# The first two columns of a norm weight fetched by GpSimd, its whole turned later, and 17 fillers in place of 13 in a one-core encoder layer

## The chip, the core and the metric

The kernel runs on one core of a Trainium2 chip. The metric is the device time of one execution in microseconds (us), taken as the median of several executions; less is better. Engines are named as the profile names them: PE (TensorE matmul) with PEld (its weight loads), DVE (VectorE), ACT (ScalarE), POOL (GpSimd) and SP (SyncE). ACT, SP and POOL also issue DMAs; a "q" behind a name (ACTq, SPq, POOLq) marks such an issue.

## What is computed

One layer of a bidirectional encoder: RMS norm, one projection, two head groups (attention and a gated linear recurrence), and an output projection with a residual. Only the beginning matters here:

```
def rms_norm(x, w):                       # x: 512 x 2048, w = norm_w: 2048
    y = x * rsqrt(mean(x * x, -1) + EPS)
    return y * w

h = rms_norm(x, norm_w)
proj = einsum('bsd,de->bse', h, w_in)     # w_in: 2048 x 4608
q, k, v, g_attn, xr, g_lru = split(proj)  # xr is projected first here
...
return x + einsum('bse,ed->bsd', mixed, w_out)
```

## The kernel before

The 2048 channels are handled in 16 blocks of 128, two blocks to a chunk `c` of 256 channels. A matmul contracts over the partitions, so each 128x128 square of x has to be turned (transposed by PE against the identity matrix `ident`) before it can be used. `xturn` (L226) turns one block: four transposes into one PSUM tile, then ACT writes the block scaled by its column of `norm_w` and rounded to the short float32 format (`xh`, L232), and DVE writes what the rounding left (`xl`, L233). The row factor of the norm is applied after the projection. `wsplit` (L198) splits a weight tile in the same way: ACT casts (`wh`, L204), DVE subtracts (`wl`, L205). Each product is then three matmuls: high x high, high x low, low x high.

The scaling needs one column of `norm_w` per block, that is, each channel's value on its own partition. Before, `norm_w` comes in as 16 rows of 128 (`nw_st`, 16 descriptors of 512 B, L937, on ACT's queue between the two halves of the first weight tile), and `columns` (L175) turns it whole with one small PE transpose (L179) and a DVE copy (L181) into `nw`, 128x16.

While nothing has arrived, PE multiplies a tile of ones with itself (`busy`, L921, the "fillers": 128x256 in bfloat16, L923): `WARM` = 13 of them at the very beginning, and `WARM2` = 6 between the first turned block and the first product. The ones are set by GpSimd (L153), behind the identity's first instruction.

PE's order is the order in which the code is written. It begins: 13 fillers, turn of `norm_w`, turn of block 0, 6 fillers, four products of block 0 (L287: high x high for four column blocks), turn of block 1, the other products of blocks 0 and 1, then chunk after chunk (L145 to L147). At the beginning ACT, DVE and SP keep the written order as well. Each waits on semaphores, in order; what stands behind a waiting instruction on its engine waits too. The lines of the setup are 934 to 955:

```
    with tc.high_priority():
        xs, ws = xload(0, 2), wraw(w_in, 0, C_XR, 2, nc.scalar)
        xc, raw = next(xs), next(ws)
        nc.scalar.dma_start(nw_st, norm_w.rearrange("(k p) -> k p", p=P))
        next(xs), next(ws)
        ...
        columns(nw, nw_st)
        first = [wsplit(raw, 0)]
        xturn(xc, 0)
        busy(WARM2)
```

`xload(0, 2)` brings chunk 0 of x in two halves of 256 KB on SP's queue (block 0, then block 1); `wraw(..., 2, nc.scalar)` brings the first weight tile in two halves of 256 KB on ACT's queue.

Of the kernel before, what the change touches and what calls it, by code (L numbers as in the profile page):

```python
# [12 lines left out]
AF = mybir.ActivationFunctionType  # L13
ALU = mybir.AluOpType
AX = mybir.AxisListType

P = 128
# [19 lines left out]
AHEAD = 600  # L37


WARM, WARM2 = 13, 6  # L40


STEPS = 2
# [12 lines left out]
def hybrid_kernel(  # L56
# [20 lines left out]
    nc = tc.nc  # L77
# [34 lines left out]
    def x2():  # L112
        return pools["xw"].tile([P, SEQ], F32R, tag="x2", bufs=32, name=nm("x2"))
# [21 lines left out]
    def mm():  # L135
        return ps.tile([P, SEQ], F32, tag="mm", name=nm("mm"))

    def const(shape, name, dt=F32):
        return cp.tile(list(shape), dt, tag=name, name=name)

    def f(ap):
        return ap.bitcast(F32)
# [7 lines left out]
    ident = const([P, P], "ident")  # L150
    make_identity(nc, ident)
    ones = const([P, P], "ones")
    nc.gpsimd.memset(ones, 1.0)  # L153
    nhalf = const([P, 48], "nhalf")
    nc.gpsimd.memset(nhalf, -0.5)

    nw_st = const([KT, P], "nw_st")
    vec_st = const([R_END, P], "vec_st")

    def vec_load():  # L160
        for lo, src in (
            (R_CW, conv_w.rearrange("t o (n p) -> (t o n) p", p=P)),
            (R_CB, conv_b.rearrange("(n p) -> n p", p=P)),
            (R_BA, lru_ba.rearrange("d (n p) -> (d n) p", p=P)),
            (R_BX, lru_bx.rearrange("d (n p) -> (d n) p", p=P)),
            (R_LAM, lru_lambda.rearrange("d (n p) -> (d n) p", p=P)),
            (R_AN, attn_norm_w.rearrange("(n p) -> n p", p=P)),
            (R_LN, lru_norm_w.rearrange("(n p) -> n p", p=P)),
        ):
            nc.sync.dma_start(vec_st[lo : lo + src.shape[0], :], src)  # L170

    nw = const([P, KT], "nw")
    vec = const([P, R_END], "vec")

    def columns(dst, src):  # L175

        n = src.shape[0]
        pt = mm()
        nc.tensor.transpose(pt[:, :n], src, ident[:n, :n])  # L179
        with tc.high_priority():  # L180
            nc.vector.tensor_copy(dst, pt[:, :n])  # L181
# [5 lines left out]
    def wraw(w, r0, c0, nk=1, queue=nc.sync):  # L187

        raw = pools["wr"].tile([P, 2, SEQ], F32, tag="wr", bufs=3, name=nm("wr"))
        src = w[r0 : r0 + 2 * P, c0 : c0 + SEQ].rearrange("(k p) e -> p k e", p=P)  # L190
        for k in range(nk):
            ks = slice(k * 2 // nk, (k + 1) * 2 // nk)
            queue.dma_start(raw[:, ks, :], src[:, ks, :])
            yield raw
# [3 lines left out]
    def wsplit(raw, k):  # L198

        turn_of[0] += k  # L200
        pool = pools["wx" if "wx" in pools and turn_of[0] % 2 else "xw"]
        hi = pool.tile([P, SEQ], F32R, tag="wh", bufs=4, name=nm("wh"))
        lo = pool.tile([P, SEQ], F32R, tag="wl", bufs=4, name=nm("wl"))
        nc.scalar.copy(hi, raw[:, k, :])  # L204
        nc.vector.tensor_sub(lo, raw[:, k, :], f(hi))  # L205
        return hi, lo

    def wload(w, r0, c0):
        with tc.high_priority(AHEAD):
            (raw,) = wraw(w, r0, c0)  # L210
            return [wsplit(raw, k) for k in range(2)]


    xh, xl = [None] * KT, [None] * KT
    ssq = const([P, NT, KT // 2], "ssq")

    def xload(c, nk=1):

        xc = b4(shape=(P, NT, 2 * P))
        for k in range(nk):  # L220
            ks = slice(k * 2 * P // nk, (k + 1) * 2 * P // nk)
            cs = slice(c * 2 * P + ks.start, c * 2 * P + ks.stop)
            nc.sync.dma_start(xc[:, :, ks], xf[:, cs].rearrange("(t p) d -> p t d", p=P))
            yield xc

    def xturn(xc, kk):  # L226
        pt = mm()
        for t in range(NT):
            ks = slice(kk % 2 * P, (kk % 2 + 1) * P)
            nc.tensor.transpose(pt[:, t * P : (t + 1) * P], xc[:, t, ks], ident)  # L230
        xh[kk], xl[kk] = x2(), x2()
        nc.scalar.activation(xh[kk], pt, AF.Identity, scale=nw[:, kk : kk + 1])  # L232
        nc.vector.scalar_tensor_tensor(  # L233
            xl[kk], pt, nw[:, kk : kk + 1], f(xh[kk]), op0=ALU.mult, op1=ALU.subtract
        )

    def xsquare(xc, c):
        for t in range(NT):
            nc.vector.scalar_tensor_tensor(
                xc[:, t, :], xc[:, t, :], 1.0, xc[:, t, :], op0=ALU.mult, op1=ALU.mult,  # L240
                accum_out=ssq[:, t, c : c + 1],
            )

    def xchunk(c):
        with tc.high_priority(AHEAD):
            (xc,) = xload(c)
        yield
        with tc.high_priority(AHEAD):
            for k in range(2):
                xturn(xc, 2 * c + k)  # L250
        xsquare(xc, c)
        yield
# [17 lines left out]
    def xstats():  # L270
        s = const([P, NT], "xsum")
        nc.vector.reduce_sum(s, ssq, axis=AX.X)
        rsqrt_mean(rstd, s, DM, NT)
        rows(rbc, rstd, k2(shape=(P, NT, P)))
# [3 lines left out]
    def proj_feat(c0, acc, first=None, given={}):  # L278

        acc += [pj() for _ in range(4)]  # L280
        for c in range(KT // 2):
            if c == 0 and first:

                for k, (wh, wl) in enumerate(first):
                    for j, (w, x_) in enumerate(((wh, xh), (wl, xh), (wh, xl))):
                        for e in range(4):
                            nc.tensor.matmul(  # L287
                                acc[e], w[:, e * P : (e + 1) * P], x_[k],
                                start=k == 0 and j == 0, stop=False,
                            )  # L290
                            if (j, e) in ((1, 1), (2, 3)):
                                yield c, 2 * k + j - 1
                        if (k, j) == (0, 0):
                            yield None
                continue
            ws = given[c] if c in given else wload(w_in, c * 2 * P, c0)
            for e in range(4):
                es = slice(e * P, (e + 1) * P)
                for k, (wh, wl) in enumerate(ws):
                    kk = 2 * c + k  # L300
                    mm3(acc[e], wh[:, es], wl[:, es], xh[kk], xl[kk], kk == 0, kk == KT - 1)
                yield c, e
# [618 lines left out]
    def busy(n):  # L921
        for _ in range(n):
            nc.tensor.matmul(warm[:, : 2 * P], wv[:, :P], wv, start=True, stop=True)  # L923
# [10 lines left out]
    with tc.high_priority():  # L934
        xs, ws = xload(0, 2), wraw(w_in, 0, C_XR, 2, nc.scalar)
        xc, raw = next(xs), next(ws)
        nc.scalar.dma_start(nw_st, norm_w.rearrange("(k p) -> k p", p=P))  # L937
        next(xs), next(ws)
        table = const([P, 1], "table")
        nc.scalar.activation(table, ones[:, :1], AF.Exp)  # L940
        columns(nw, nw_st)
        first = [wsplit(raw, 0)]
        xturn(xc, 0)
        busy(WARM2)
    chunks = [xchunk(c) for c in range(1, KT // 2)]
    loads, turns = iter(chunks), iter(chunks)
    for step in proj_feat(C_XR, a1, first, given):
        if step is None:
            with tc.high_priority():
                first.append(wsplit(raw, 1))  # L950
                xturn(xc, 1)
            xsquare(xc, 0)
            next(next(loads), None)
            given[1] = wload(w_in, 2 * P, C_XR)
            continue
        c, e = step
        if (e == 0 or e == 2) and c:
            next(next(loads, iter(())), None)
        if (e, c) == (2, 0) or (e == 1 and c) or (e, c) in ((3, 1), (3, 2)):
            next(next(turns, iter(())), None)  # L960
        if (c, e) == (1, 2):
            given[2] = wload(w_in, 4 * P, C_XR)
            s2.close()
        if (c, e) == (2, 3):
            vec_load()
        if (c, e) == (5, 3):
            columns(vec, vec_st)
        if (c, e) == (KT // 2 - 1, 0):
            with tc.high_priority():
                xstats()  # L970
# [171 lines left out]
```

## Time and profile before

| | us |
|---|---|
| three executions | 663.28, 663.50, 661.22 |
| median | 663.28 |
| the profiled execution: its own time | 663.34 |
| the profiled execution: span, first to last instruction | 661.5 |

So 1.8 us of the profiled execution's time lie outside its span. Every time below counts from the start of that span. PE is busy for 654.1 us of the span in 3067 matmuls, DVE 490.6, ACT 346.0, POOL 91.8. A row of the timeline reads: start, duration, engine, line, operation, output<-inputs, shapes, count, and in brackets the idle time of the engine before it with what ended it. Rows of one kind that follow each other are merged into one (x13). A matmul's duration runs from its issue to its modelled end, so durations of neighbours overlap; the pace is read from starts, or from the chain of waits, which has no overlaps.

### The profile page before, as it was taken

What the parts mean: (1) busy time and instruction counts of PE and PEld (TensorE: products, weight loads), DVE (VectorE), ACT (ScalarE), POOL (GpSimd) and SP (SyncE); (2) the same over time, 40 slices, a digit from 0 to 9 for tenths busy, and PEclk for the clock granted to TensorE, in tenths of its full rate; (3) what the DMA queues carried; (4) which work ended last, traced back from release to release, by engine and by line L of the source; (5) the groups of instructions that cost most, each with busy time, mean ns of one, the idle gap of its engine ahead of it and who ended that gap; (6) DMA issues with size and microseconds to landing.
All of it is one profiled execution on the core that took longest, in us unless ns stands there. A gap on an engine that the chain in (4) does not pass through costs nothing.

```text
span 661.5 us, 8826 instructions
## 1 busy us (share of the span) xinstructions
PE 654.1 (99%) x3067; PEld 540.6 (82%) x3067; DVE 490.6 (74%) x851; ACT 346.0 (52%) x639; POOL 91.8 (14%) x121
## 2 busy tenths in 40 slices
PE   8999999999999999999999999999999999999997
PEld 6888888888888888888888888888888878888875
DVE  4879688977687952855865569528967998698994
ACT  3543799489856514454644437435444564333441
POOL 0000000000012301223253335410000000010000
PEclk9999999999999999999999999999999999999999
DMA  8843252322334221345776768762355766585322
GB/s 289 272 143 96 65 141 90 97 64 64 83 106 151 81 90 32 97 138 149 152 168 164 216 128 180 176 153 79 89 164 207 264 215 216 211 290 192 125 83 95
DMA packets 52732, 96.19 MB, mean 145 GB/s; under 512 B 4184, under 2 KB 14544, under 8 KB 52560
## 3 DMA queue, kind: packets, MB, share of 16 engines
q1 hardware_dynamic: 45648, 75.17, 36.0%
q0 software_dynamic: 6720, 19.93, 13.1%
q10 hardware_dynamic: 320, 0.53, 0.3%
q8 instruction: 24, 0.39, 0.2%
q14 instruction: 20, 0.16, 0.1%
HBM read 91.42 MB, written 20.97 MB: 170 GB/s over the span
## 4 chain that ended last, share of the span: by engine, by line
PE 88%; DVE 4%; issue 3%; DMA 3%; POOL 1%; ACT 0%; DVEq 0%; ACTq 0%; POOLq 0%
PE pj L145 19%; PE pj L147 19%; PE pj L146 19%; PE mm L890 9%; PE pj L890 7%; PE mm L146 3%; PE mm L147 3%; PE mm L145 3%; DVE ol L705 2%; PE mm L575 2%; DMA rw<-ts 2%; PE mm L230 1%; PE pj L287 1%; PE mm L523 1%; DMA nw_st<-in_norm_w_dram 1%
## 5 line engine op out<-in xcount | busy, mean ns | idle before, releaser
L145 PE MATMUL pj<-x,wh 128*128 128x512 f32 x376 | 150.2, 400 | 0.0
L147 PE MATMUL pj<-x,wl 128*128 128x512 f32 x376 | 147.1, 391 | 0.0
L146 PE MATMUL pj<-x,wh 128*128 128x512 f32 x376 | 146.7, 390 | 0.0
L204 ACT CAST wh<-wr 128x512 fp32r<-128x512 f32 x144 | 86.5, 617 | 75.9 <-PE pj L147 29.0
L205 DVE TENSOR_TENSOR wl<-wr,wh 128x512 fp32r<-128x512 f32 x144 | 99.5, 711 | 30.7 <-ACT wh L204 30.5
L147 PEld LDWEIGHTS pj<-x,wl 128*128 128x128 f32 x376 | 70.6, 188 | 15.4
L146 PEld LDWEIGHTS pj<-x,wh 128*128 128x128 f32 x376 | 70.8, 188 | 14.0 <-issue 0.5
L145 PEld LDWEIGHTS pj<-x,wh 128*128 128x128 f32 x376 | 70.7, 188 | 13.8 <-issue 0.5
L145 PE MATMUL pj<-wh,x 128*128 128x512 f32 x192 | 75.7, 394 | 0.0
L146 PE MATMUL pj<-wl,x 128*128 128x512 f32 x192 | 75.3, 392 | 0.0
L147 PE MATMUL pj<-wh,x 128*128 128x512 f32 x192 | 75.2, 392 | 0.0
L704 ACT CAST oh<-rw 128x512 fp32r<-128x512 f32 x94 | 54.8, 619 | 31.8 <-PE mm L890 14.5
L705 DVE TENSOR_TENSOR ol<-rw,oh 128x512 fp32r<-128x512 f32 x94 | 60.6, 686 | 9.2 <-ACT oh L704 6.8
L890 PE MATMUL mm<-ol,mh 128*128 128x512 f32 x128 | 50.2, 392 | 0.5 <-DVE ol L705 0.5
L890 PE MATMUL mm<-oh,mh 128*128 128x512 f32 x128 | 50.3, 393 | 0.0
L890 PE MATMUL mm<-oh,ml 128*128 128x512 f32 x128 | 50.2, 392 | 0.0
L577 ACT CAST b<-mm 128x512 fp32r<-128x512 f32 x32 | 18.7, 585 | 58.7 <-PE mm L575 58.7
L563 DVE TENSOR_REDUCE mx<-mm 128x1 f32<-128x512 f32 x32 | 22.0, 688 | 31.2 <-PE mm L147 30.9
L145 PEld LDWEIGHTS pj<-wh,x 128*128 128x128 f32 x192 | 36.1, 188 | 8.1 <-issue 0.2
L146 PEld LDWEIGHTS pj<-wl,x 128*128 128x128 f32 x192 | 36.1, 188 | 8.1 <-issue 0.2
L147 PEld LDWEIGHTS pj<-wh,x 128*128 128x128 f32 x192 | 36.1, 188 | 7.9
L890 PE MATMUL pj<-oh,mh 128*128 128x512 f32 x96 | 37.8, 394 | 0.0
(207 smaller groups left out, 1153.7 us busy)
## 6 DMA issues: line engine op xcount, KB each, us to landing
wr<-in_w_in_dram SPq DMA_DIRECT2D x71, 512.0 KB, 3.7
rw<-in_w_out_dram SPq DMA_DIRECT2D x63, 256.0 KB, 3.9
ts<-in_w_out_dram POOLq DMA_DIRECT2D x24, 512.0 KB, 6.9
rw<-ts SPq DMA_DIRECT2D x31, 256.0 KB, 5.0
ts<-ts POOLq DMA_DIRECT2D x8, 512.0 KB, 5.7
xt<-in_x_dram SPq DMA_DIRECT2D x8, 512.0 KB, 8.2
b<-in_x_dram SPq DMA_DIRECT2D x7, 512.0 KB, 7.7
out_dram<-xt POOLq DMA_DIRECT2D x12, 256.0 KB, 3.0
```

The lines of the kernel that those rows point to most:

```text
L145: nc.tensor.matmul(acc, lh, rh, start=start, stop=False)
L146: nc.tensor.matmul(acc, lh, rl, start=False, stop=False)
L147: nc.tensor.matmul(acc, ll, rh, start=False, stop=stop)
L204: nc.scalar.copy(hi, raw[:, k, :])
L205: nc.vector.tensor_sub(lo, raw[:, k, :], f(hi))
L230: nc.tensor.transpose(pt[:, t * P : (t + 1) * P], xc[:, t, ks], ident)
L563: nc.vector.tensor_reduce(mx, sc, axis=AX.X, op=ALU.max, negate=True)
L575: nc.tensor.transpose(pt[:, s * P : (s + 1) * P], p[:, s * P : (s + 1) * P], ident)
L577: nc.scalar.copy(pth[:, :, tt], p3)
L704: nc.scalar.copy(hi, src)
L705: nc.vector.tensor_sub(lo, src, f(hi))
L890: nc.tensor.matmul(bank[name, s], lh[:, a, ts_], rh, start=i == 0 and j == 0, stop=i == 7 and j == 2,)
```

## The change

- `nw2`, a new 128x2 tile, takes the first two columns of `norm_w` straight from memory: GpSimd issues a DMA of 128x2 single elements (256 pieces of 4 bytes). Blocks 0 and 1 are scaled with `nw2`, all others with `nw` as before.
- `norm_w` as 16 rows (`nw_st`) is issued behind the second half of the first weight tile on ACT's queue; its turn and copy (`columns`) stand behind the turn of block 1.
- `WARM` is 17 in place of 13.
- The ones are set by VectorE instead of GpSimd.

```
-WARM, WARM2 = 13, 6
+WARM, WARM2 = 17, 6
...
-    nc.gpsimd.memset(ones, 1.0)
+    nc.vector.memset(ones, 1.0)
...
     nw = const([P, KT], "nw")
+    nw2 = const([P, 2], "nw2")
...
-        nc.scalar.activation(xh[kk], pt, AF.Identity, scale=nw[:, kk : kk + 1])
+        w = (nw2 if kk < 2 else nw)[:, kk : kk + 1]
+        nc.scalar.activation(xh[kk], pt, AF.Identity, scale=w)
         nc.vector.scalar_tensor_tensor(
-            xl[kk], pt, nw[:, kk : kk + 1], f(xh[kk]), op0=ALU.mult, op1=ALU.subtract
+            xl[kk], pt, w, f(xh[kk]), op0=ALU.mult, op1=ALU.subtract
         )
...
         xc, raw = next(xs), next(ws)
+        nc.gpsimd.dma_start(nw2, norm_w[: 2 * P].rearrange("(k p) -> p k", p=P))
+        next(xs), next(ws)
         nc.scalar.dma_start(nw_st, norm_w.rearrange("(k p) -> k p", p=P))
-        next(xs), next(ws)
         table = const([P, 1], "table")
         nc.scalar.activation(table, ones[:, :1], AF.Exp)
-        columns(nw, nw_st)
         first = [wsplit(raw, 0)]
...
                 first.append(wsplit(raw, 1))
                 xturn(xc, 1)
+                columns(nw, nw_st)
```

What stands in a row on the engines is shown at three places. A row reads: line, operation, output<-inputs, shape, and the semaphores that it waits for; DMAHW0, DMAHW1, ... count the transfers of the SP and ACT queues in turn, eight counts that are used again, and DMASW0 that of GpSimd. Line numbers of the changed kernel are one to three higher.

The first place is PE's start. Before, from the last filler of the first group to the first filler of the second; `b_18_139` is chunk 0 of x:

```order
L923 MATMUL mm_118<-ones 128x256
L179 MATMUL mm_148<-ident,nw_st 128x16 [waits DMAHW2_49,Pool_49]
L230 MATMUL mm_155<-ident,b_18_139 128x128 [waits DMAHW1_49]
L230 MATMUL mm_155<-ident,b_18_139 128x128 x3
L923 LDWEIGHTS ones
```

Now the same stretch:

```order
L925 MATMUL mm_119<-ones 128x256
L231 MATMUL mm_158<-ident,b_18_144 128x128 [waits DMAHW1_49,Pool_49]
L231 MATMUL mm_158<-ident,b_18_144 128x128 x3
L925 LDWEIGHTS ones
L925 MATMUL mm_119<-ones 128x256
```

And PE now from the last of the first four products of block 0 on (`mm_185` is block 1 turned):

```order
L289 MATMUL pj_176<-x_23_163,wh_154 128x512
L231 MATMUL mm_185<-ident,b_18_144 128x128 [waits DMAHW3_49]
L231 MATMUL mm_185<-ident,b_18_144 128x128 x3
L180 MATMUL mm_194<-ident,nw_st 128x16 [waits DMAHW4_49]
L289 MATMUL pj_173<-x_23_163,wl_155 128x512 [waits DVE_49]
```

The turn of `nw_st` has left the place ahead of block 0, and with it the wait for its transfer; it now stands behind the turn of block 1, ahead of the products with `wl`.

The second place is ACT's start. Before:

```order
L193 DMA wr_141<-in_w_in_dram 128x512
L937 DMA nw_st<-in_norm_w_dram 16x128
L193 DMA wr_141<-in_w_in_dram 128x512
L940 ACT_TABLE_LOAD
L940 ACTIVATE table<-ones 128x1 [waits Pool_49]
L204 CAST wh_151<-wr_141 128x512 [waits DMAHW0_49]
L232 ACTIVATE x_24_160<-mm_155,nw 128x512 [waits DVE_49,PE_49]
L204 CAST wh_178<-wr_141 128x512 [waits DMAHW4_49]
```

Now; `nw_93` is `nw2`:

```order
L194 DMA wr_146<-in_w_in_dram 128x512 x2
L941 DMA nw_st<-in_norm_w_dram 16x128
L943 ACT_TABLE_LOAD
L943 ACTIVATE table<-ones 128x1 [waits DVE_49]
L205 CAST wh_154<-wr_146 128x512 [waits DMAHW0_49]
L234 ACTIVATE x_23_163<-mm_158,nw_93 128x512 [waits DMASW0_49,PE_49]
L205 CAST wh_181<-wr_146 128x512 [waits DMAHW2_49]
```

`nw_st` is issued third instead of second, and the scaling of block 0 waits for GpSimd's transfer where it waited for DVE's copy.

The third place is POOL's start. Before:

```order
masks.py:197 MEMSET ident 128x128
L153 MEMSET ones 128x128
masks.py:199 ISA
masks.py:199 AFFINE_SELECT ident<-ident 128x128 [waits Pool_49]
L155 MEMSET nhalf 128x48
```

Now:

```order
L939 DMA nw_93<-in_norm_w_dram 128x2x1
masks.py:197 MEMSET ident 128x128
L155 MEMSET nhalf 128x48
masks.py:199 ISA
masks.py:199 AFFINE_SELECT ident<-ident 128x128 [waits Pool_49]
```

The DMA stands ahead of the identity, and the memset of the ones is gone from here; it is now DVE's first instruction.

## The prediction

> **What bounds the kernel now.** I read the shares by engine first, then the chain of waits of the first 16 us in order of time, then single engines. From the page:
>
> ```profile
> PE 654.1 (99%) x3067; PEld 540.6 (82%) x3067; DVE 490.6 (74%) x851; ACT 346.0 (52%) x639; POOL 91.8 (14%) x121
> PEclk9999999999999999999999999999999999999999
> PE 88%; DVE 4%; issue 3%; DMA 3%; POOL 1%; ACT 0%; DVEq 0%; ACTq 0%; POOLq 0%
> ```
>
> PE holds 88% of the chain, so a microsecond that PE gains at the start is carried to the end, unless something behind it is not ready. The change touches only the start. The chain there (start, duration, what):
>
> ```profile
> 0.72 0.45 ACTq L193
> 1.17 0.03 issue
> 1.20 4.21 DMA nw_st<-in_norm_w_dram
> 5.41 0.14 issue
> 5.54 0.26 PE mm L179
> 5.80 1.05 PE mm L230 x4
> 6.84 1.28 PE mm L923 x6
> 8.12 1.71 PE pj L287 x4
> 9.83 0.54 PE mm L230 x4
> 10.37 3.23 PE pj L287 x14
> 13.60 0.87 PE mm L230 x8
> 14.47 1.38 PE pj L287 x6
> ```
>
> Two things are to be seen. The norm weight's rows, issued at 1.20, land at 5.41, and PE starts on them alone. And the pace doubles: four products take 1.71 us (0.43 each), the 14 after 10.37 take 3.23 (0.23 each); four turns take 1.05, then eight 0.87. The rise lies near 9.9. The page's clock row shows 9 in every slice, so it does not show this; the paces do.
>
> Now PE and ACT themselves, by the timeline:
>
> ```profile
> 1.12 2.95 PE L923 MATMUL mm<-ones 128*128 128x256 bf16 x13 [1.12 <-POOL ones L153]
> 5.54 0.26 PE L179 MATMUL mm<-ident,nw_st 16*128 16x16 f32 x1 [1.46 <-DMA nw_st<-in_norm_w_dram]
> 5.73 1.12 PE L230 MATMUL mm<-ident,b 128*128 128x128 f32 x4
> 7.78 2.06 PE L287 MATMUL pj<-x,wh 128*128 128x512 f32 x4
> 13.44 1.04 PE L230 MATMUL mm<-ident,b 128*128 128x128 f32 x8
> 19.21 0.48 PE L145 MATMUL pj<-x,wh 128*128 128x512 f32 x1
> ```
>
> ```profile
> 6.88 0.69 ACT L232 ACTIVATE x<-mm,nw 128x512 fp32r<-128x512 f32 x1 [1.66 <-PE mm L230]
> 7.47 0.61 ACT L204 CAST wh<-wr 128x512 fp32r<-128x512 f32 x1
> 14.07 1.27 ACT L232 ACTIVATE x<-mm,nw 128x512 fp32r<-128x512 f32 x2 [1.95 <-PE mm L230]
> ```
>
> PE is busy from 1.12 to 4.07, idle for 1.46, then busy without a break. So 2.95 us of work without a break did not bring the rise, and the 4.3 to 4.4 us from 5.54 on did.
>
> **Part 1: the first turn starts earlier.** When is x there? SP's rows:
>
> ```profile
> 5.02 0.51 SPq L193 DMA_DIRECT2D wr<-in_w_in_dram  x1
> 8.12 2.15 SPq L170 DMA_DIRECT2D vec_st<-in_conv_w_dram  x1
> b<-in_x_dram SPq DMA_DIRECT2D x2, 256.0 KB, 4.6
> ```
>
> The DMA at 5.02 waits, by the program, for the same count (DMAHW1) as PE's turn of block 0. So block 0 is there by 5.0, and nw_st by 5.4 was the last. From landing to PE went 0.13 (5.41 to 5.54). The earliest new start is 5.1. Against it stand 256 extra pieces and a second weight half that now follows the first without nw_st between; nothing in the trace shows their price. The bounds are nothing and what block 1 shows, 4.6 us from its issue near 1.2, so 5.8. I take 5.25, nearest to the row that is the same transfer: 0.48 earlier than 5.73.
>
> **Part 2: 17 fillers and VectorE's ones.** GpSimd's row for the ones is 0.20 from 0.86, behind the identity's; on DVE nothing is ahead, so 0.72 + 0.20, and PE starts near 1.0 instead of 1.12.
>
> ```profile
> 0.72 0.20 POOL masks.py:197 MEMSET ident<- 128x128 f32 x1 [0.29 <-POOLq L1127]
> 0.86 0.20 POOL L153 MEMSET ones<- 128x128 f32 x1
> 1.36 0.13 POOL L155 MEMSET nhalf<- 128x48 f32 x1
> ```
>
> At 2.95/13 = 0.227 each, 17 take 3.86 and end at 4.85, before the turn at 5.25: they delay nothing, and the gap shrinks from 1.46 to 0.4. If the rise needs L us of unbroken work, L lies between 2.95 and 4.4. Fillers of 3.86 reach it over 0.91 of these 1.45 us, and if a gap of 0.4 does not undo what went before, everywhere: the rise comes between 1.0 + 2.95 = 3.95 and 1.0 + 4.4 + 0.4 = 5.8. This is the larger term.
>
> **Part 3: the sum** at the fast pace, row by row. Turn at 5.25; ACT's scaling 0.63 later (13.44 to 14.07), at 5.88; it ends at 6.57 (0.69); the first product 0.2 later (before: 7.57 to 7.78), at 6.77. Six fillers fit in between, since they need half of 1.28. Four products: 0.25 for the first (0.48 against 0.23, row 19.21) and 4 x 0.23; turn of block 1, half of 0.87; turn of nw_st, 0.2 (5.54 to 5.73). That is 6.77 + 0.25 + 0.92 + 0.44 + 0.2 = 8.58, where before it was 10.37: 1.79 less. With the rise only at 5.8, turn and scaling go at the old distance (5.73 to 6.88, 1.15), and it is about 1.3 less. I take **1.7**, near the first, since most of 3.95 to 5.8 lies before the turn.
>
> **Part 4: what must be hidden.** The new transfer, first of all. The groups of GpSimd's DMAs (count; busy, mean ns), then the landing times by line, in the same order:
>
> ```profile
> L738 POOL DMA_DIRECT2D ts<-in_w_out_dram x16 | 17.4, 1089 | 49.3 <-issue 39.5 <-DVE ev L632 4.8 <-DVE mx L563 4.8
> L735 POOL DMA_DIRECT2D ts<-in_w_out_dram x8 | 6.2, 780 | 2.8 <-issue 2.8
> L825 POOL DMA_DIRECT2D out_dram<-xt x12 | 6.6, 554 | 197.3 <-DVE xt L861 145.9 <-DMA rw<-in_w_out_dram 23.4 <-DVE xt L866 23.2
> DMA to landing us min/median/max: 6.3/7.2/8.9
> DMA to landing us min/median/max: 3.9/4.9/8.4
> DMA to landing us min/median/max: 2.5/2.9/5.6
> ```
>
> L735 and L738 move 512 KB in 256 rows, as many pieces as nw2 has (L738 adds to what is there); the stores, L825, 256 KB in 128 rows. nw2 has 1 KB. ACT needs it at 5.88, that is 5.16 after its issue at 0.72. Bounds: 2.5 to 8.9; I take 4, above the stores' median since it has twice the pieces among busy queues, and below L735's since few bytes are to be moved: there at 4.7, with 1.2 to spare. The identity waits behind this issue: 0.72 + 1.09 at most + the 0.77 of the rows from 0.72 to 1.49 makes 2.6, under the fillers; without that cover it would cost 1.9.
>
> A price that only the notes state: the Trainium skill, "DMA: Bandwidth & Descriptors" (Anatomy of one DMA), gives about 2 us fixed for a DMA issued by GpSimd, so about 2.7 as an estimate; no run here has such a small one, and the sum would stay the same.
>
> nw_st now lands behind the second weight half. That half is there by 8.12 (the load of vec_st waits for it) and by ACT's cast at 7.47; its issue is 0.55 earlier now. nw_st is needed at 8.4. Bounds: nothing, or a few tenths if it comes after 8.4; I take nothing. DVE's copy (0.17) moves in between; its first reader, ACT's scaling of chunk 1, comes at 14.07 - 1.8 = 12.3, about 2 us after. SP's load of chunk 4 now waits for the weight half, at most 2 us later than 5.57; chunk 4 is turned at 25.7. Choosing nw2 or nw is free.
>
> The profiled execution took 663.34, of which 661.5 is span: 663.34 - 1.7 = **661.6**. The median, 663.28, is the same within 0.06.
>
> **Rivals.**
>
> *The rise does not come earlier* (chance 0.24). If it needs more than 3.86 us and any gap starts it anew, it comes 4.3 after the new start, as before. Then only the start remains: 0.48 less, 662.9. For it: one break of 1.46 did undo 2.95 us of work. Against it: most of the values of L that the trace allows are below 3.86. The Trainium skill, "TensorE: Matmul & The Clock Gate" (Part 1), has a rule that speaks for this rival: the rise follows a window of 3.4 us at a phase free of the kernel's start that was busy throughout. By that, 3.86 us hold a whole window in about one start of eight; by its wording of a busy window with a threshold it does not name, more. The rise at 9.9 agrees with such windows, and does not tell the threshold.
>
> *The small transfer is late* (slower; 0.09). Its place is ACT L232, with the cast of the second weight half queued behind it, and all products behind both. Landing after L738's longest, 8.9, is 9.62: ACT starts 2.74 later than at 6.88. If the faster pace is there by then, four products give 0.8 back: +1.9, 665.2. It decides from a landing at 6.9 on the span's clock without the early rise, at 7.7 with it. For it: 4-byte pieces among queues that are full. Against it: the stores' median of 2.9.
>
> *It does not do what it says* (0.08): pushed by the new pieces, block 0 comes at 5.6 or later, the gap is 0.8 or more and the rise stays: 663.3.
>
> **How the numbers follow.** Forecast 0.55, with a range of its own from 661.3 to 662.4. About 0.04 is left for causes that I don't see. The range from 660.2 to 664.0 takes in the forecast and the rivals at 662.9 and 663.3; below, it allows for scatter, one execution of before having been 2 us under the others; the late transfer is left out. A measurement of this kernel tells about 0.5% (3.3 us) from no change. No case gives 3.3 us less by its rows: the whole wait and the whole slow pace are hardly more than 2.3; scatter leaves 0.06 for faster. Slower by 3.3 needs a landing at 10 or later: 0.03. Within 0.5%: 0.91.
>
> **What would show it.** First turn of block 0 between 5.1 and 5.5, with at most 0.6 of idle time before it, ended by the transfer of x: part 1. The first four products in about 0.95 on the chain, not 1.71: part 2; if they take 1.7, the first rival. ACT's first scaling released by PE: part 4 right; by the DMA of nw2: the second. The block of 14 products starting near 8.6. PE waiting at the turn of nw_st, or at chunk 1 for DVE, would make the prediction wrong in a way that I priced at nothing.

## The result, and the profile after

| | median, us | all executions, us | ratio to before |
|---|---|---|---|
| before, in the same job | 663.11 | 661.22 to 664.40 (22) | |
| the changed kernel | 663.88 | 663.70 to 665.59 (22) | 1.0019 [1.0012, 1.0025] |

The change costs 0.8 us: within 0.5% of before, but on the other side of it than the forecast of 661.6. The executions of the changed kernel fall in two groups, 17 of 22 at 663.7 to 664.0 and 5 at 665.3 to 665.6; the profiled one (665.36, span 663.6) belongs to the second. No execution of the first group was traced, so what sets the two apart can only be argued from other kernels' traces, below.

The chain of waits of its start (start, duration, what):

```profile
1.29 5.96 DMA nw<-in_norm_w_dram
...
7.34 0.70 ACT x L234
...
8.08 1.97 PE pj L289 x4
10.05 0.85 PE mm L231 x4
10.90 0.21 PE mm L180
11.12 3.67 PE pj L289 x14
```

It begins with the small transfer, `nw2` (the profile leaves out the numbers in names and writes `nw`). Its issue starts at 1.29, not at 0.72, it lands at 7.25, and ACT's first scaling waits for it. The four products take 1.97 and the 14 products start at 11.12; before, it was 10.37.

PE and ACT by the timeline:

```profile
1.04 3.81 PE L925 MATMUL mm<-ones 128*128 128x256 bf16 x17 [1.04 <-DVE ones L153]
5.36 0.63 PE L231 MATMUL mm<-ident,b 128*128 128x128 f32 x4 [0.51 <-DMA b<-in_x_dram]
5.82 0.82 PE L925 MATMUL mm<-ones 128*128 128x256 bf16 x6
8.08 1.97 PE L289 MATMUL pj<-x,wh 128*128 128x512 f32 x4 [1.44 <-ACT x L234]
```

```profile
7.34 0.69 ACT L234 ACTIVATE x<-mm,nw 128x512 fp32r<-128x512 f32 x1 [2.22 <-DMA nw<-in_norm_w_dram]
```

Everything up to the first turn is as forecast. The fillers run from 1.04 to 4.85, and block 0 is turned at 5.36 after a gap of 0.51 that x's transfer ends. The turn takes 0.63 where it took 1.12, and six fillers take 0.82, so the fast pace is there. Then ACT sits idle for 2.22 and PE for 1.44. And the pace is lost again, as the windows show (first column the window, last three the granted clock, the DMA share, which is printed a little above 1 where the engines are full, and GB/s):

```profile
8.00:9.00 1.00, 0.92 (x3) 0.73 (x4) 0.94 (x2) 0.53 (x2) 0.00 (x0) 0.61 1.04 380
9.00:10.00 1.00, 1.00 (x4) 0.70 (x3) 0.41 (x1) 0.00 (x0) 0.00 (x0) 0.50 1.09 356
...
11.00:12.00 1.00, 1.00 (x4) 0.82 (x5) 0.34 (x1) 1.00 (x2) 0.00 (x0) 0.68 1.10 354
```

The clock is at half between two changes: 0.61 over the first microsecond puts the fall at 8.22, and 0.68 over the last the rise at 11.64. The clock records that are kept with the trace have the same two, and an earlier rise at 4.81.

### The profile page after: what moved, and what is told of

The parts are those of the page before. It is cut to its first block, busy times and chain, and to the rows that moved or that the text cites. A ratio compares the mean times of both kernels' runs of the same rounds, so it can differ in the third digit from the quotient of the medians.

```text
span 663.6 us, 8840 instructions
## 1 busy us (share of the span) xinstructions
PE 655.9 (99%) x3071; PEld 540.5 (81%) x3071; DVE 491.0 (74%) x852; ACT 346.5 (52%) x639; POOL 93.0 (14%) x121
## 4 chain that ended last, share of the span: by engine, by line
PE 96%; DMA 1%; DVE 1%; issue 1%; ACT 0%; DVEq 0%; ACTq 0%; POOLq 0%
PE pj L147 20%; PE pj L145 20%; PE pj L146 20%; PE mm L892 12%; PE pj L892 9%; PE mm L147 3%; PE mm L146 3%; PE mm L145 3%; PE mm L577 2%; PE pj L289 1%; PE mm L231 1%; DMA nw<-in_norm_w_dram 1%; PE mm L525 1%; DMA rw<-in_w_out_dram 1%; DVE ol L707 0%
## 5 line engine op out<-in xcount | busy, mean ns | idle before, releaser
L892 PE MATMUL pj<-ol,mh 128*128 128x512 f32 x96 | 37.8, 394 | 0.0
```

The source lines that it names most:

```text
L892: nc.tensor.matmul(bank[name, s], lh[:, a, ts_], rh, start=i == 0 and j == 0, stop=i == 7 and j == 2,)
```

## The experiments

Theory: the gains of the forecast came, and two costs ate them, the late transfer and one outside the start. Rivals: the early pace does not come or is worth nothing; or moving `nw_st` or GpSimd's part of the work costs something of its own. Each job timed the kernel before beside its kernels; "against before" is the difference to that median. Line numbers of after hold for its variants; those of before, for its variants (one more where a tile is added).

**a1_ones_scale.** The changed kernel with blocks 0 and 1 scaled by ones (it leaves `norm_w` out of these two blocks); the transfer is issued, and nobody waits for it.

```
-        w = (nw2 if kk < 2 else nw)[:, kk : kk + 1]
+        w = ones[:, :1] if kk < 2 else nw[:, kk : kk + 1]
```

> The changed kernel, with blocks 0 and 1 scaled by a column of ones instead of nw2: the norm weight is left out for these two blocks, the small DMA is still issued and nobody waits for it. Theory A (the late landing of nw2, 7.25 us in the changed kernel, ate the gain): ACT's first scaling starts within 0.7 us of the turn's start, near 6.0, the chain's 14 products start near 8.7 instead of 11.1, no fall of the clock, and the time is about 1.7 us under the kernel before: ratio 0.997 to 0.998. Rival B (the fillers or the 256 pieces cost the time themselves, by the clock or by pushing x): ACT starts early, and yet the time stays within 0.5 us of before or above.

Measured: 662.49 (662.17 to 662.99, 11 executions), before 662.89, ratio 0.9997 [0.9989, 1.0006]. Its chain:

```profile
0.73 4.15 DMA b<-in_x_dram
...
5.01 0.65 PE mm L231 x4
...
5.68 0.70 ACT x L234
...
6.42 1.21 PE pj L289 x4
...
8.06 0.16 PE mm L180
8.22 3.40 PE pj L289 x14
```

This is the start that the forecast worked out: x's transfer first, then no wait but ACT's scaling; the turn of `nw_st` waits for nothing. The 14 products start at 8.22 (forecast 8.58; before 10.37). Yet of these 2.15 us the median keeps 0.40, which cannot be told from nothing. Something after the start takes back well over 1 us.

**a2_before_17.** The kernel before with 17 fillers, nothing else.

```
-WARM, WARM2 = 13, 6
+WARM, WARM2 = 17, 6
```

> The kernel before with 17 fillers and nothing else. Theory of the clock (unbroken work of about 3.4 us brings the rise; short breaks do not undo it): the rise comes before 6 us in most executions, the four first products take 0.95 us on the chain, and the time is 1.0 to 1.4 us under before, ratio 0.998 to 0.9985. Rival (the earlier rise is lost again in the gap between the fillers and the first product, as in the changed kernel's profile): ratio 0.9995 to 1.001, with a fall of the clock in the profile.

Measured: 662.79, before 662.89, ratio 0.9996 [0.9985, 1.0006], in two groups: 5 of 12 executions at 661.3 to 661.7, 7 at 662.6 to 663.6. The profiled one, 661.40, is of the first:

```profile
1.17 4.18 DMA nw_st<-in_norm_w_dram
...
5.69 0.60 PE mm L230 x4
...
7.06 1.20 PE pj L287 x4
...
8.69 3.21 PE pj L287 x14
```

With `nw_st` still the last to land, the fast pace alone brings the 14 products from 10.37 to 8.69. But 7 of 12 executions did not gain, and none of them was traced, so why is open. The kernel before has a low group too: in this job 5 of its 29 executions took 661.3 to 661.8. The four fillers may have made that group more frequent; the two medians cannot be told apart.

**a3_nw2_act.** The 256 pieces on ACT's queue instead, between the halves of the first weight tile.

```
-        nc.gpsimd.dma_start(nw2, norm_w[: 2 * P].rearrange("(k p) -> p k", p=P))
+        nc.scalar.dma_start(nw2, norm_w[: 2 * P].rearrange("(k p) -> p k", p=P))
```

> The changed kernel with nw2 fetched in the same 256 pieces by ACT's queue, between the two halves of the weight tile, instead of by GpSimd. If GpSimd's way of issuing makes nw2 late: it lands near 5.4, as nw_st did there, ACT scales at about 6, and the time is 1 to 1.7 us under before (ratio 0.9975 to 0.9985). If it is the 4-byte pieces among full queues: it lands at 7 or later again, and the ratio is 1.000 to 1.003.

Measured: 662.61 (662.58 to 663.36, 11), ratio 0.9996 [0.9988, 1.0005]. The profiled execution is the slowest of them (663.36; the other ten lie between 662.58 and 662.76):

```profile
5.03 1.09 PE L231 MATMUL mm<-ident,b 128*128 128x128 f32 x4 [0.17 <-DMA b<-in_x_dram]
```

```profile
6.15 0.69 ACT L234 ACTIVATE x<-mm,nw 128x512 fp32r<-128x512 f32 x1 [0.97 <-PE mm L231]
```

```profile
2.35 6.91 DMA nw_st<-in_norm_w_dram
...
9.53 3.38 PE pj L289 x14
```

By this queue `nw2` is in time; ACT's scaling is released by PE. But `nw_st`, queued behind it, now takes 6.91 from its issue, where it took 5.4 in the changed kernel, and its turn becomes the wait: here the pieces moved the wait, and did not remove it. The first turn is slow although 17 fillers ended just 0.17 before it. (This kernel also carries the cost that p1 finds, so its time is not that of the start alone.)

**a4_after_13.** The changed kernel with 13 fillers.

```
-WARM, WARM2 = 17, 6
+WARM, WARM2 = 13, 6
```

> The changed kernel with 13 fillers as before. If the late nw2 is the whole cost and the four fillers bring little because the clock's early rise is wasted or falls again: ratio to before 1.001 to 1.003, as the changed kernel. If the 17 fillers were worth their 1.2 us even with the late nw2: 1.003 to 1.005. If the fillers cost time themselves (a rise too early that falls again): under the changed kernel, 0.9995 to 1.0015.

Measured: 666.16 (665.34 to 666.29, 5), ratio 1.0045 [1.0033, 1.0057]. The profiled execution, 665.34:

```profile
5.18 0.63 PE L231 MATMUL mm<-ident,b 128*128 128x128 f32 x4 [1.17 <-DMA b<-in_x_dram]
```

```profile
11.07 3.67 PE pj L289 x14
```

Against before the median is +3.27, where the changed kernel has +0.77, so with the late transfer the four more fillers are worth 2.5 us. The trace does not show them at work, though: here too the first turn is fast, and the 14 products start at 11.07, as in the changed kernel's profile (11.12), which took 665.36. All five executions are like that kernel's second group or slower, so the fillers seem to change how often the pace is kept. That is argued from the groups, and not traced.

**p1_before_pad.** The kernel before with the tile `nw2` and nothing that uses it. Tiles are laid out one behind the other, in steps of 32 bytes; in the built programs this tile moves tiles behind it (x, the first weights and their halves among them) from addresses that are multiples of 64 bytes in a partition to 32 behind one.

```
     nw = const([P, KT], "nw")
+    nw2 = const([P, 2], "nw2")
```

> The kernel before with one unused 128x2 tile where nw2 would stand, so that every tile behind it lies 32 bytes further; no instruction differs. Theory of the layout (the slower pace of products, 229.3 ns from start to start in all kernels with nw2 against 228.8 without, comes of the shift by 32 bytes): pace 229.3, time 1.0 us above before, ratio 1.001 to 1.002. Rival (the pace comes of the transfers or the order of the changed kernel, or differs from execution to execution): pace 228.8, ratio 0.9995 to 1.0005.

Measured: 663.88 (662.53 to 664.45, 11), before 662.83, ratio 1.0015 [1.0006, 1.0024]: a tile that nobody touches costs 1.05 us (by the interval, 0.4 to 1.6). Where, can be read in a stretch in which PE never rests, between two marks of the chain: eight turns of chunk 7, and 16 small products of the first attention block. Before, then this kernel, then the changed one:

```profile
39.43 0.87 PE mm L230 x8
...
233.89 1.68 PE mm L643 x16
```

```profile
39.61 0.87 PE mm L231 x8
...
234.56 1.68 PE mm L644 x16
```

```profile
40.65 0.87 PE mm L231 x8
...
235.61 1.68 PE mm L645 x16
```

The stretch takes 194.46, then 194.95 and 194.96. Half a microsecond is lost over some 850 products (194.46 / 0.228), 0.6 ns on each; over the 512-column products from 20 us on, the mean distance from start to start (distances under 300 ns) is 228.74 ns before, 229.36 here and 229.35 in the changed kernel. The loss is not even. Set beside the same products of before, p1's are 0.16 us late at 23 us, 0.69 at 298 us, 0.38 at 549 us and 1.0 at the end: it builds up in the first 300 us and behind 550 us, and not in between. (The step back by 0.3 near 430 us is this trace of before: a2 and b2, whose tiles are not moved, show it against that trace as well.)

**p2_after_64.** The changed kernel with the two columns in a tile of 64 bytes a partition, so that the tiles behind it keep multiples of 64.

```
-    nw2 = const([P, 2], "nw2")
+    nw2 = const([P, 16], "nw2")[:, :2]
```

> The changed kernel with nw2 as two columns of a 128x16 tile, so that all tiles behind it lie 64 bytes further than before instead of 32. Theory of the layout: pace 228.8, the time 1.0 us under the changed kernel (663.9), so 662.8, ratio to before 0.9995 to 1.0003; the landing of nw2 stays at about 7.2 us. Rival: pace 229.3, ratio 1.001 to 1.002 as the changed kernel.

Measured: 662.27 (662.15 to 663.93, 11), ratio 0.9997 [0.9988, 1.0006]; 1.6 less than the changed kernel.

```profile
1.29 5.96 DMA nw<-in_norm_w_dram
...
8.08 1.19 PE pj L289 x4
...
9.87 3.40 PE pj L289 x14
...
39.08 0.87 PE mm L231 x8
...
233.27 1.68 PE mm L645 x16
```

The stretch takes 194.19, so the loss is gone (mean distance 228.62 ns). And this is a start with the same landing, 7.25, in which the pace stays: the four products at 8.08 take 1.19 and the 14 start at 9.87. It is the best picture here of the changed kernel's first group; two of its own 11 executions lie 1.5 higher, like that kernel's second.

**c2_ones_64.** The edits of a1 and p2 together (`norm_w` is left out of two blocks).

> The changed kernel with blocks 0 and 1 scaled by ones (leaves norm_w out of these two blocks; the small transfer is issued, and nobody waits for it), and with nw2 as two columns of a 64-byte tile, so that the tiles behind it lie on the addresses of before (mod 64). Theory A (the late transfer and the shift of 32 bytes are two terms that add up, and without both the forecast of 661.6 holds): 661.2 to 661.8. Rival B (the shift cost is only worth something where the start is late): 662.3 to 662.6, as with the shift (662.49). Rival C: below 661.0, more than the two terms.

Measured: 660.74 (660.54 to 661.20, 5), before 663.04, ratio 0.9967 [0.9954, 0.9980]. The four kernels, against before in their own jobs:

| | tiles 32 bytes further | tiles on multiples of 64 |
|---|---|---|
| ACT waits for nw2 | +0.77 (changed kernel) | -0.56 (p2) |
| nobody waits for it | -0.40 (a1) | -2.30 (c2) |

The wait is worth 1.2 to 1.7, the addresses 1.3 to 1.9, and the change loses by having both. Without either it gains 2.3, somewhat more than the forecast's 1.7 and a little under the bound of 661.0 that the expectation gave for that. A part of the excess can be read: c2's 14 products start at 8.32, where the forecast had 8.58, and in p2 the stretch above is 0.27 shorter than before's, so 64 bytes more is a little better than before's own addresses; why is open. The wait is worth 0.6 more in one column than in the other, about as much as these ratios are uncertain, so whether the terms add up exactly stays open.

**b2_row_pool.** Why is GpSimd's transfer late? The kernel before, with its 16 rows of 512 bytes fetched by GpSimd in place of ACT.

```
-        nc.scalar.dma_start(nw_st, norm_w.rearrange("(k p) -> k p", p=P))
+        nc.gpsimd.dma_start(nw_st, norm_w.rearrange("(k p) -> k p", p=P))
```

> The kernel before with the 16 rows of 512 bytes fetched by GpSimd instead of ACT, nothing else. If GpSimd's way makes the transfer late whatever its pieces: it lands near 7 and the time rises by 1 to 2 us, ratio 1.0015 to 1.003. If the 256 pieces of 4 bytes make it late: these 16 rows land by 5.4 and the time is within 0.5 us of before.

Measured: 663.78 (662.38 to 665.09, 11), ratio 1.0016 [1.0007, 1.0025].

```profile
1.29 5.09 DMA nw_st<-in_norm_w_dram
...
6.52 0.25 PE mm L179
```

The same transfer lands at 6.38 in place of 5.41, between the two expectations: it starts 0.09 later than on ACT's queue (1.20) and takes 5.09 in place of 4.21. The 256 pieces take another 0.87 (5.96). So both GpSimd's way and the pieces have a part, at a time when the queues are full. The kernel's time says less here, since GpSimd also sets the ones behind this DMA: the fillers start at 2.34 in place of 1.12.

**b3_quiet and b4_full.** The changed kernel, with the same transfer issued once more into a third tile, when it is quieter (behind the row sums of x) or while loads still fill the queues (behind the turn of `norm_w`). Of each:

```
+                nw3 = const([P, 2], "nw3")
+                nc.gpsimd.tensor_scalar(nw3, rstd[:, :2], 1.0, 0.0, op0=ALU.mult, op1=ALU.add)
+                nc.gpsimd.dma_start(nw3, norm_w[: 2 * P].rearrange("(k p) -> p k", p=P))
```

(in b4 with `nw[:, :2]` in place of `rstd[:, :2]`).

> The changed kernel, and GpSimd's transfer of 128x2 elements is issued a second time into a third tile, after the row sums of x are done (near 40 us), when few loads are under way. Only the second transfer's landing is read. Theory A (what the way through GpSimd takes for such a transfer, 256 pieces of 4 bytes, is long in itself): it lands 5 to 6 us after its issue begins, as the first did (5.96). Rival B (the first was late because all queues were full of x and the first weights): it lands 2.5 to 3.5 us after its issue begins, like the median of this kernel's stores (2.9).

> The changed kernel, and GpSimd's transfer of 128x2 elements is issued a second time into a third tile right behind the turn of norm_w (near 12 us), while loads still keep the DMA engines 90% busy or more. Only the second transfer's landing is read; near 46 us, where the DMA engines were 41% busy, it took 3.2, at the start 6.0. Theory A (full queues make it late): 5 to 6.5 us from its issue. Rival B (only the first transfer that GpSimd issues is slow, whatever the queues do): 3 to 3.5.

Measured, one execution each: 663.25 and 662.19. The second issue, and its landing time by line, in b3:

```profile
45.86 0.80 POOL L976 DMA_DIRECT2D nw<-in_norm_w_dram  x1 [0.30 <-POOL nw L975]
DMA to landing us min/median/max: 3.2/3.2/3.2
```

and in b4:

```profile
11.80 0.77 POOL L957 DMA_DIRECT2D nw<-in_norm_w_dram  x1 [0.30 <-POOL nw L956]
DMA to landing us min/median/max: 6.0/6.0/6.0
```

By the windows of each (DMA share and GB/s last), the DMA engines are full around b4's second issue and not around b3's. First b4, with a transfer of 8 KB that SP issues at this time and its landing time; then b3:

```profile
10.00:14.00 4.00, 4.00 (x23) 3.38 (x22) 3.41 (x12) 1.67 (x4) 1.06 (x2) 1.00 1.08 361
...
vec_st<-in_lru_ba_dram SPq DMA_DIRECT2D x1, 8.0 KB, 6.7
```

```profile
45.00:50.00 5.00, 5.00 (x24) 4.10 (x23) 2.80 (x10) 1.93 (x4) 1.27 (x3) 1.00 0.41 113
```

The same transfer takes 3.2 us at 46 us of the span and 6.0 at 12, and at 12 a small one of SP's takes 6.7. So most of the lateness goes with the full queues, and neither with GpSimd alone nor with the first use of its queue. These are single executions.

**b1_row_first and c1_row_first_13.** If the row is the last to land, issue it first: the kernel before with `nw_st` ahead of the first weight half on ACT's queue, and ones by VectorE; 17 fillers (b1) or 13 (c1). No `nw2`.

```
     with tc.high_priority():
         xs, ws = xload(0, 2), wraw(w_in, 0, C_XR, 2, nc.scalar)
-        xc, raw = next(xs), next(ws)
         nc.scalar.dma_start(nw_st, norm_w.rearrange("(k p) -> k p", p=P))
+        xc, raw = next(xs), next(ws)
         next(xs), next(ws)
```

> The kernel before with the norm weight's 16 rows issued first on ACT's queue, 17 fillers and the ones set by VectorE; no nw2, so no shift of the tiles. If the sum of the prediction was right for what it counts (early turn, early rise): the turn of nw_st near 4.9 is hidden, block 0 is turned from 5.2 on, ACT scales near 6, and the time is 661.3 to 661.8, ratio 0.9975 to 0.9985. If the first weight half, now second on its queue, becomes the bound, or the rise comes early in half of the executions only: 662.3 to 662.8, ratio 0.999 to 1.000.

> The kernel before with nw_st issued first on ACT's queue and the ones set by VectorE, but 13 fillers. Theory A (the order of the two issues is worth its own part, and the early rise of the pace comes mainly from 17 fillers): about 662.3, that is 0.5 below before, and with 17 fillers it was 661.3. Rival B (with the row first the gap is short enough that 13 fillers do as well): 661.3, as with 17. Rival C (the order is worth nothing without the fillers): 662.8, as before.

Measured: b1 661.30 (660.80 to 661.57, 11), before 662.83, ratio 0.9978 [0.9969, 0.9987]; c1 661.48 (661.10 to 662.82, 9), before 663.04, ratio 0.9983 [0.9971, 0.9995]. Both beat the kernel before and the changed one, and the two cannot be told apart. From the issues and the timeline of c1:

```profile
nw_st<-in_norm_w_dram ACTq DMA_DIRECT2D x1, 8.0 KB, 2.4
```

```profile
1.04 2.96 PE L923 MATMUL mm<-ones 128*128 128x256 bf16 x13 [1.04 <-DVE ones L153]
3.93 0.28 PE L179 MATMUL mm<-ident,nw_st 16*128 16x16 f32 x1
4.14 1.11 PE L230 MATMUL mm<-ident,b 128*128 128x128 f32 x4
5.05 1.49 PE L923 MATMUL mm<-ones 128*128 128x256 bf16 x6
6.76 1.21 PE L287 MATMUL pj<-x,wh 128*128 128x512 f32 x4 [0.23 <-ACT x L232]
```

Issued first, the row lands in 2.4 us, before the 13th filler ends, and PE goes from filler to turn without a gap. The fast pace is there by 6.76 without any more fillers. I had expected the fillers to matter here. What bounds this start instead is the first weight half, now second on its queue, and its cast, behind which ACT's scaling stands; b1, then c1:

```profile
5.84 0.62 ACT L204 CAST wh<-wr 128x512 fp32r<-128x512 f32 x1 [2.02 <-DMA wr<-in_w_in_dram]
```

```profile
5.50 0.62 ACT L204 CAST wh<-wr 128x512 fp32r<-128x512 f32 x1 [1.68 <-DMA wr<-in_w_in_dram]
```

In b1 the turn is fast (0.66), and PE then waits 1.18 for ACT; the products start at 7.10 there and at 6.76 in c1. This wait was named in b1's expectation as the way to fail; it came, and the time was still as hoped.

## Why the prediction was wrong, point by point

**The times of parts 1 to 3 held, the reason given in part 2 did not.** The first turn came at 5.36 in the changed kernel and 5.01 in a1 (5.25 forecast, with 5.1 to 5.8 as bounds: a1 is just below), the fillers ended at 4.85 as worked out, the turn of block 0 was already fast, and without the late transfer the 14 products started at 8.22, earlier than 8.58. The first rival, that the rise does not come earlier, is refuted in every traced start with 17 fillers; the latest is a3's, where the first turn still took 1.09 and only the four products, from 6.97 on, were fast (1.17). But part 2 took a length of unbroken work, between 2.95 and 4.4 us, that 17 fillers would reach and 13 not. In a4's profile 13 fillers, with a gap of 1.17 behind them, were enough, and in a3's 17 were too few for the first turn: the clock records have the rise at 4.71 and 6.89, the latter behind the forecast's last moment, 5.8. The fillers do help: by the first turn the pace is fast in 8 of 9 traced starts with 17 and in 1 of 5 with 13. But a length of work alone does not decide it, and to that extent the changed kernel's early rise was luck. That most executions have it is not shown either: a2 gained in 5 of 12 only.

**Two steps failed. The first is Part 4's landing of nw2**, "there at 4.7, with 1.2 to spare". It landed at 7.25, 2.55 later. 0.57 of that is the start of the issue, at 1.29 and not where POOL's first memset stood before (0.72). The other 1.96 is the duration, 5.96 for 4. The bounds (2.5 to 8.9) held it; the choice within them was wrong. I put it near the stores' 2.9 because few bytes move, but those stores run late in the kernel. In b3 and b4 the same 1 KB took 3.2 and 6.0, by how full the queues were. A row from the same time in the kernel was there, `nw_st`'s 4.21, and it had 16 pieces, not 256. The Trainium skill, "DMA: Bandwidth & Descriptors" (Anatomy of one DMA), with its 2 us fixed, was further off. Another section of that page of the Trainium skill (Latency and other measured facts) says that the fixed part shrinks when the memory is less loaded; the direction agrees with 3.2 against 6.0.

**By the second rival's own rule this would not yet have made it slower.** The prediction said that a late transfer decides from a landing at 7.7 if the pace is fast by then. 7.25 is before that, and p2, with that landing, is at -0.56 of before (not to be told from 0). So the wait eats most of the gain of 1.7, as rows: 9.87 against a1's 8.22, and 10.37 before. What that rival missed is that the longer idle time can undo the pace. Probably that is why 5 of 22 executions end 1.5 us later; the profiled one, which is of these, shows the clock at 0.50 from 8.22 to 11.64.

**The second step, which turned the sign, was not in the sum at all.** "Choosing nw2 or nw is free" was argued of the instructions that read the tile. The tile's place was not looked at: its 32 bytes move x and the weights behind it, and p1 shows that this alone costs 1.05 us of the whole program. No term, no bound and no rival spoke of it. It is also why the chain of the first 16 us, on which I relied, could not hold the whole answer: most of the loss lies behind 23 us, in amounts of 0.6 ns. Added up, the forecast's gain of 1.7, the wait's 1.65 and this 1.05 make +1.0, against +0.77 measured.

**What was hidden stayed hidden.** `nw_st` behind the second weight half delayed nothing in a1 or the changed kernel (PE's turn of it, L180, follows the turn of block 1 directly); the identity, done at 2.79 by POOL's rows, was under the fillers.

## What to carry to other kernels

A small transfer costs what the queues make it wait, so price it from a row of the same moment, and put the one that is needed first ahead in its queue (b1, c1) before making it smaller or giving it to another engine. A new tile is not free because nothing waits for it: look at what its size does to the addresses of the matmul operands behind it, and undo that shift (p2) before judging a change by a few tenths of a per cent. With the row issued first, 17 fillers did not beat 13 (b1, c1): close the gap before filling it.

## What the runs showed of the hardware

**Operands off a multiple of 64 bytes.** 512-column products whose tiles lie 32 bytes behind a multiple of 64 start every 229.35 ns in place of 228.74 (p1, a1, a3, a4 and the changed kernel: 229.32 to 229.36; before, a2, b1, b2 and c1: 228.72 to 228.78; p2, b3, b4 and c2, 64 bytes further: 228.58 to 228.64; one trace each). Which of the operands it is, wasn't tried.

**The clock moves in steps of 3.4 us, and in both directions.** In the changed kernel's profile it rises at 4.81, falls at 8.22 and rises at 11.64, each 3.41 or 3.42 after the one before. The window from 4.81 to 8.22 held 1.95 us of idle time (0.51 and 1.44) and the clock fell. In p2, with gaps of 0.58 and 1.69, the record has the rise at 4.06, so that its windows are cut elsewhere, and the clock stayed:

```profile
8.00:9.00 1.00, 0.92 (x4) 0.79 (x5) 0.94 (x2) 0.54 (x2) 0.00 (x0) 1.00 1.02 388
```

So about 57% of idle time in one such window was enough for the fall, and the 49% (1.66 us) of p2's window from 4.06 to 7.47 were not. If such windows also run ahead of the first rise, the same working gives the share that brings it: in a4, work for 79% of the window that ends with the rise at 4.71 was enough, and in a3, 71% of the window that ends 3.41 before the rise at 6.89 was not. The Trainium skill, "TensorE: Matmul & The Clock Gate" (Part 1), gives windows of 3413 ns whose phase is independent of the kernel's start; the steps agree, and the different fate of the same start in different executions fits a free phase, which these runs do not prove. The Trainium skill's budget for idle time (the same Part 1: back to the slow rate after an idle window) would be misread here if taken as a gap of a whole window: 1.95 us in two gaps sufficed.
